# Feed-forward of a hybrid decoder layer: seven-product blocks for gate and up, a spilled hidden layer, and front work put on ScalarE

## Chip, core and metric

One core of one Trainium2 chip runs the whole step as one program. The metric is the device time of one execution in microseconds (us), the median of several. PE is TensorE, PEld its weight loads, DVE is VectorE, ACT is ScalarE, POOL is GpSimd, SP is SyncE, which issues all the DMAs here.

## What is computed

One decoder layer on 1056 tokens (1024 of a prompt, 32 sample tokens), width 1024, all in float32: an input projection, a recurrent branch (convolution of width 4, gated linear recurrence) beside windowed attention, group norms, an output projection, a layer norm, then a gated feed-forward of width 2816 and a second layer norm.

```python
log_a = -LRU_C * r.astype(jnp.float32) * jax.nn.softplus(-lru_lambda.astype(jnp.float32))
a = jnp.exp(log_a)
u = jnp.sqrt(-jnp.expm1(2.0 * log_a)) * (i * x).astype(jnp.float32)
...
h1 = layer_norm(ALPHA * x + y_mix, ln1_g, ln1_b)
hid = jax.nn.silu(jnp.einsum('bsd,df->bsf', h1, w_gate)) * jnp.einsum('bsd,df->bsf', h1, w_up)
ffn = jnp.einsum('bsf,fd->bsd', hid, w_down)
h2 = layer_norm(ALPHA * h1 + ffn, ln2_g, ln2_b)
```

`r` and `i` are sigmoids of two small block products of the convolved `x`.

## The kernel before, in words

**Tokens and tiles.** Activations lie feature-major, [128 features, tokens]. The tokens are two chunks (`SC`): chunk 0 has 512, chunk 1 has 544, and chunk 1 is worked in two blocks of 272 (`BL`), so that a product has 512 or 272 columns. A weight unit is [128, 1024]. Every float32 operand is split into two float32r parts, high and low, and a product is three matmuls (`three`, line 589): high by high, high by low, low by high. One unit against all tokens is thus 8 x 3 x 3 = 72 matmuls, 24 with 512 columns and 48 with 272.

**Splitting a unit.** `split_unit` (line 542) takes each half of a unit, 128x512: a copy to float32r (`copy`, ACT first, DVE possible), and a subtraction for the low part (`tt`, POOL first, DVE possible). A half of a `w_down` unit has its rows' means taken off as well: a sum on DVE, an ACT instruction and a DVE instruction.

**Order.** The program records its instructions, and a list scheduler (`Recorder.order`, line 263) then puts them in the order of issue, by what each costs in a model of its own, by the data and buffers it waits for, and by a latest start worked out backwards from TensorE's order (`deadlines`, line 241). An instruction that two engines can do (`either`, line 204) goes to the first named, unless that would be late and the other is done sooner (`leave`, line 313). Each engine then runs its own list strictly in order; SP too, so a DMA that waits holds up the DMAs behind it.

**Front, lines 606 to 1250.** Projections, recurrence and attention of both chunks, then `out_stream` (line 1222) of chunk 0 and of chunk 1. `attend` (line 849) masks and exponentiates scores, and divides by the sum on DVE (line 878). `recurrence` (line 1046) does the four taps of the convolution on DVE, and adds the gates' biases on DVE (line 1071); `scans` (line 1077) takes the sigmoids, an exponential, a tanh and a square root on ACT. `gate_stream` (line 1129) adds its bias on DVE.

**Middle.** `layer_norm1` (line 1253) normalizes each block, splits the result into `h1` (`finish1`, line 1288), sums it over the features (`add_sum`, line 1244) and takes off the mean, for the second norm. The first three feed-forward tiles (`AHEAD`) are done for chunk 0 alone while chunk 1 is normalized, and afterwards for chunk 1 alone.

**Feed-forward.** `gate_up` (line 1297) does one tile f of 128 hidden features: a gate product into `ps_fg`, silu on ACT, an up product into `ps_fu`, their product on DVE, and a split into `hid`. After each two tiles `down` (line 1331) adds their share of all 8 output tiles to `y1`, through `ps_d`, so that down products lie between gate and up products. All of `h1` and `y1` and a few tiles of `hid` stay in SBUF, in 73 slots of [128, 544] (`NSLOT`). `last_down` and `norm2` (lines 1338 and 1355) finish block by block.

Of the kernel before, what the change touches and what calls it, by code (L numbers as in the profile page):

```python
# [17 lines left out]
P = 128  # L18
# [17 lines left out]
NSLOT2 = 10  # L36
NPR = 4
STEP = 2500
AHEAD = 3
# [13 lines left out]
# ---- a small list scheduler: the kernel below records its instructions; they are issued in the order in which they  # L53
# can run, given what each engine costs per instruction (shapes only), the data they wait for and the free buffers
# [32 lines left out]
class Tag:  # L87
    def __init__(self, pool, kind, cap):
        self.pool, self.kind, self.cap, self.psum = pool, kind, cap, pool.psum
        self.bufs, self.free, self.first = [], cap, 0  # L90

# [58 lines left out]
class Recorder:  # L150
# [5 lines left out]
    def add(self, engine, fn, args, kw, *others):  # L156
        """`others`: (engine, function, args, kw) of instructions that would do the same on another engine"""
# [58 lines left out]
    @contextlib.contextmanager  # L216
    def batch(self):
        """instructions that are to run one after the other: each waits for the data of all"""
        self.group = []
        yield  # L220
        waits = set().union(*(op.before for op in self.group)) - set(self.group)
        for op in self.group:
            op.before |= waits
        self.group = None

    def extra(self, b):
        """how many buffers the instructions recorded before b's may still need beside those in use"""
        t = b.tag
        ev = []
        for c in t.bufs[t.first : b.order]:  # L230
            if not c.taken:
                ev.append((c.start, 1))
                ev.append((c.end + 0.5, -1))
        ev.sort()
        n = peak = 0
        for _, d in ev:
            n += d
            peak = max(peak, n)
        return peak
# [23 lines left out]
    def order(self):  # L263
# [41 lines left out]
        def finish(op, e):  # L305
            """when engine e would be through with op after the more urgent work that waits for it"""
# [17 lines left out]
        def dispatch(e):  # L324
# [34 lines left out]
            for b in op.bufs:  # L359
                if not b.taken:  # L360
                    b.taken = True
                    t = b.tag
                    t.free -= 1
                    while t.first < len(t.bufs) and t.bufs[t.first].taken:
                        t.first += 1
# [62 lines left out]
def cost(engine, fn, outs, ins, args, kw):  # L428
    """ns of an instruction, from its shape"""
# [23 lines left out]
def hybrid_step(ctx: ExitStack, tc: tile.TileContext, xT, w_in, w_gates, w_out, w_g, w_u, w_d, vec, ck, cv, ck_nat,  # L453
# [17 lines left out]
    late = {}  # L471
# [4 lines left out]
    def temp(name):  # L476
        if "pool" in late:
            return late["pool"].tile([P, 512], F32, tag="g2", name=name, bufs=NSLOT2)
# [5 lines left out]
    # ---- constants and small vectors  # L484
    vt = const.tile([P, NVEC], F32, tag="vt", name="vt")
    oi = const.tile([P, 2 * P], F32, tag="oi", name="oi")
    mk = const.tile([P, 2 * P], F32, tag="mk", name="mk")
# [10 lines left out]
    # ---- emission: a queue of matrix work fills the tensor engine between the steps of the other work  # L498
# [16 lines left out]
    def run_filler(stream, step):  # L515
        """emit the stream; after each `step` ns of its matmuls advance the other work"""
# [7 lines left out]
    # ---- weights: a unit is [128, 1024], split exactly into two float32r parts, prefetched in order of use  # L524
# [6 lines left out]
    def load(j):  # L531
        """raw halves of unit j"""
        if state["raw"] == j and j < len(units):
            src, name, _ = units[j]
# [7 lines left out]
    def split_unit(j):  # L542
        if state["part"] == j and j < len(units):
            _, name, halves = units[j]
            if halves:
                h = [slot(f"{name}_h{i}", F32R, HW) for i in range(2)]
                l = [slot(f"{name}_l{i}", F32R, HW) for i in range(2)]
                hs_, ls_ = h, l
            else:
                h = pw.tile([P, D], F32R, tag="wh", name=f"{name}_h", bufs=2)  # L550
                l = pw.tile([P, D], F32R, tag="wl", name=f"{name}_l", bufs=2)
                hs_, ls_ = ([q[:, i * HW : (i + 1) * HW] for i in range(2)] for q in (h, l))
            if halves:
                # less each row's mean over its columns: the second layer norm would take it off their sums
                c = small.tile([P, 4], F32, tag="c", name=f"{name}_c", bufs=3)
                for i in range(2):
                    nc.vector.reduce_sum(c[:, i : i + 1], raws[j][i], axis=mybir.AxisListType.X)
                nc.vector.tensor_scalar(c[:, 2:3], c[:, 0:1], c[:, 1:2], -1.0 / D, op0=ALU.add, op1=ALU.mult)
                for i in range(2):
                    nc.scalar.activation(hs_[i], raws[j][i], AF.Identity, bias=c[:, 2:3])  # L560
                    nc.vector.scalar_tensor_tensor(ls_[i], raws[j][i], c[:, 2:3], hs_[i].bitcast(F32), op0=ALU.add,
                                                   op1=ALU.subtract)
            else:
                for i in range(2):
                    nc.copy(hs_[i], raws[j][i])
                    nc.tt(ls_[i], raws[j][i], hs_[i].bitcast(F32), op=ALU.subtract)
# [3 lines left out]
    def need(i):  # L570
        """unit i; at its first use the next unit is split and the one after that loaded"""
        if i not in seen:
# [5 lines left out]
            if i + 1 < len(units) and units[i + 1][2]:  # L578
                load(i + 2)
                split_unit(i + 2)  # L580
                load(i + 3)
# [3 lines left out]
    def add_unit(src, name, halves=False):  # L585
        units.append((src, name, halves))
# [9 lines left out]
    def block(ps, u, xs, o, n, kts=range(KT)):  # L596
        """one [128, n] block of a projection: unit u against feature-major activations xs"""
# [89 lines left out]
    e_, s_, s2, poly, sp8, nsp8, ab, _ = (sp[:, i] for i in range(8))  # L687
# [4 lines left out]
    bcen = ng2[:, 0:8]  # L692
    def small_vectors():
# [854 lines left out]
```

## Time and profile before

| what | value |
|---|---|
| median of 3 runs | 1209.53 us (1209.03 to 1210.03) |
| span of the profiled execution | 1207.1 us; no other time of it is given |
| PE / PEld busy | 95% / 85% |
| DVE / ACT / POOL busy | 52% / 36% / 41% |
| DMA | 80.42 MB, mean 67 GB/s |

The profile is of one execution. Nearly all instructions carry line 417, the scheduler's issuing line, so a group is told by its tile names: `ps_fg`, `ps_fu`, `ps_d`, `ps_o` are the accumulators of gate, up, down and output products. PE's busy time is modelled: a 272-column matmul is shown as 0.29 us, while the next one starts 0.125 us later. What a matmul costs in a dense row is therefore read from start to start.

### The profile page before, as it was taken

Reading aid. Unit: us, or ns where it says so; the run is one execution under the profiler, and the core shown is the slowest. Engines: PE = TensorE matmul, PEld = TensorE weight load, DVE = VectorE, ACT = ScalarE, POOL = GpSimd, SP = SyncE. Lnnn points to the kernel's source line nnn. Section 1 sums busy time; section 2 is a strip of 40 time slices with the busy share of each in tenths; the row PEclk is TensorE's granted clock in tenths of the full one; section 3 lists DMA queues with packets and bytes.
Section 4 is the critical chain, followed back from the end, with each engine's and each line's share of the span. In section 5 each row is a group of like instructions: output and inputs, shape, how many; then the busy total and the mean of one; then the engine's idle time right before and its main releaser. Section 6 shows DMA issues by size and latency. Waiting matters only on the chain.

```text
span 1207.1 us, 18093 instructions
## 1 busy us (share of the span) xinstructions
PE 1147.1 (95%) x7024; PEld 1023.9 (85%) x7024; DVE 631.5 (52%) x1259; ACT 431.3 (36%) x878; POOL 491.1 (41%) x493
## 2 busy tenths in 40 slices
PE   9788998788888999999999999999999999999996
PEld 7568898776668979999898998989999899999986
DVE  5999889899977577252324142232415132232135
ACT  5375666567545375311120212113021211202135
POOL 6843476666556978412031222203031221303241
PEclk9899999899989999999999999999999999999998
DMA  8410113243121223211011111111111110202004
GB/s 291 136 53 19 41 49 101 65 142 117 63 89 54 80 78 129 90 36 53 26 63 35 53 53 45 44 36 53 36 65 41 53 44 27 70 19 70 1 1 144
DMA packets 48085, 80.42 MB, mean 67 GB/s; under 512 B 8144, under 2 KB 12400, under 8 KB 47984
## 3 DMA queue, kind: packets, MB, share of 16 engines
q1 hardware_dynamic: 48000, 79.27, 19.8%
q8 instruction: 55, 0.90, 0.3%
q14 instruction: 30, 0.25, 0.1%
HBM read 71.98 MB, written 5.58 MB: 64 GB/s over the span
## 4 chain that ended last, share of the span: by engine, by line
PE 73%; DVE 17%; DMA 3%; issue 2%; ACT 2%; POOL 2%; SPq 1%; DVEq 0%; POOLq 0%; ACTq 0%
PE ps_d L417 21%; PE ps_fg L417 20%; PE ps_fu L417 20%; PE ps_o L417 4%; DVE p L417 3%; PE ps_gt L417 3%; DVE xc L417 2%; DVE y L417 1%; DVE yat L417 1%; DVE qst L417 1%; SPq L417 1%; DVE hs L417 1%; DVE pl L417 1%; DMA x_r<-in_dram 1%; DVE v L417 1%
## 5 line engine op out<-in xcount | busy, mean ns | idle before, releaser
L417 POOL TENSOR_TENSOR wg_l<-wg_r,wg_h 128x512 fp32r<-128x512 f32 x50 | 64.8, 1311 | 344.4 <-ACT wg_h L417 344.4
L417 DVE SCALAR_TENSOR_TENSOR y<-y,ps_d 128x272 f32<-128x272 f32 (+1 forms) x240 | 124.9, 521 | 107.2 <-PE ps_d L417 102.5
L417 PE MATMUL ps_fg<-h_h,wg_l 128*128 128x272 f32 (+1 forms) x528 | 171.7, 325 | 0.4 <-POOL wg_l L417 0.4
L417 PE MATMUL ps_fg<-h_h,wg_h 128*128 128x272 f32 (+1 forms) x528 | 171.6, 325 | 0.0
L417 PE MATMUL ps_fg<-h_l,wg_h 128*128 128x272 f32 (+1 forms) x528 | 171.4, 325 | 0.0
L417 PE MATMUL ps_d<-hid_h,wd_l 128*128 128x272 f32 (+1 forms) x528 | 171.3, 325 | 0.0
L417 DVE TENSOR_REDUCE wd_c<-wd_r 128x1 f32<-128x512 f32 x44 | 30.0, 682 | 269.3 <-DMA wd_r<-in_dram 269.3
L417 PE MATMUL ps_fu<-h_h,wu_l 128*128 128x272 f32 (+1 forms) x528 | 170.7, 323 | 0.0
L417 PE MATMUL ps_fu<-h_h,wu_h 128*128 128x272 f32 (+1 forms) x528 | 170.6, 323 | 0.0
L417 PE MATMUL ps_d<-hid_h,wd_h 128*128 128x272 f32 (+1 forms) x528 | 170.6, 324 | 0.0
L417 PE MATMUL ps_d<-hid_l,wd_h 128*128 128x272 f32 (+1 forms) x528 | 170.4, 324 | 0.0
L417 PE MATMUL ps_fu<-h_l,wu_h 128*128 128x272 f32 (+1 forms) x528 | 170.4, 323 | 0.0
L417 POOL TENSOR_TENSOR hid_l<-sg,hid_h 128x272 fp32r<-128x272 f32 (+1 forms) x66 | 63.3, 960 | 126.0 <-ACT hid_h L417 108.3
L417 ACT ACTIVATE sg<-ps_fg 128x272 f32<-128x272 f32 (+1 forms) x66 | 30.5, 463 | 232.4 <-PE ps_fg L417 232.4
L417 PEld LDWEIGHTS ps_fg<-h_h,wg_l 128*128 128x128 f32 x528 | 99.8, 189 | 8.5 <-POOL wg_l L417 0.6
L417 PEld LDWEIGHTS ps_fg<-h_l,wg_h 128*128 128x128 f32 x528 | 99.5, 189 | 7.9
L417 PEld LDWEIGHTS ps_fg<-h_h,wg_h 128*128 128x128 f32 x528 | 99.8, 189 | 7.7
L417 PEld LDWEIGHTS ps_d<-hid_h,wd_l 128*128 128x128 f32 x528 | 99.2, 188 | 8.2 <-issue 0.2
L417 PEld LDWEIGHTS ps_d<-hid_h,wd_h 128*128 128x128 f32 x528 | 99.2, 188 | 8.0 <-issue 0.2
L417 PEld LDWEIGHTS ps_fu<-h_l,wu_h 128*128 128x128 f32 x528 | 99.3, 188 | 7.8
L417 PEld LDWEIGHTS ps_d<-hid_l,wd_h 128*128 128x128 f32 x528 | 99.2, 188 | 7.9
L417 PEld LDWEIGHTS ps_fu<-h_h,wu_l 128*128 128x128 f32 x528 | 99.3, 188 | 7.7
(346 smaller groups left out, 2553.1 us busy)
## 6 DMA issues: line engine op xcount, KB each, us to landing
wg_r<-in_dram SPq DMA_DIRECT2D x50, 256.0 KB, 2.6
wu_r<-in_dram SPq DMA_DIRECT2D x50, 256.0 KB, 2.6
wd_r<-in_dram SPq DMA_DIRECT2D x44, 256.0 KB, 2.6
wo_r<-in_dram SPq DMA_DIRECT2D x32, 256.0 KB, 2.6
wq_r<-in_dram SPq DMA_DIRECT2D x16, 256.0 KB, 3.6
wx_r<-in_dram SPq DMA_DIRECT2D x12, 256.0 KB, 3.5
x_r<-in_dram SPq DMA_DIRECT2D x8, 272.0 KB, 4.6
y<-in_dram SPq DMA_DIRECT2D x8, 272.0 KB, 3.4
```

The costliest lines, as they stand in the source:

```text
L417: getattr(getattr(self.nc, op.eng), op.fn)(*[real(a) for a in op.args], **{k: real(v) for k, v in op.kw.items()})
```

## The change

Two things are done. **Front:** the division in the attention, the first tap of the convolution and the gate branch's bias may now be done by ACT (first named) or DVE. The sigmoids become tanh of half the argument, taken straight from PSUM on ACT with the bias; the formulas after them carry the factors. The product by the square root names POOL first. **Feed-forward:** a pair of tiles, 2 x 128 hidden features, is one block product of 2x2 blocks (features f and f+1; halves of the 1024 inputs; halves of a chunk's tokens), done with seven products and the sums that go with them (`products`). The token-side factors are made once per chunk (`right_factors`), the weight-side ones per pair (`Pair`). All gate and up products come first; `hid` goes to DRAM, and so does the normalized `y1`. The down products follow as a stage of their own (`last_sums`): for each token block, for each half of the outputs, all 22 tiles are accumulated in four banks, and each piece of `w_down` is loaded and split again for each block. `EARLY` = 2 means that one pair is done for chunk 0 alone and then for chunk 1 alone.

```diff
-TABLES = {"Sigmoid": "sigmoid", "Sqrt": "sqrt", "Gelu_apprx_tanh": "gelu", "Silu": "silu", "Exp": "exp"}
+TABLES = {"Sigmoid": "sigmoid", "Sqrt": "sqrt", "Gelu_apprx_tanh": "gelu", "Silu": "silu", "Exp": "exp", "Tanh": "exp"}
...
+    def scaled(p, r):
+        nc.either(("scalar", "activation", (p, p, AF.Identity), dict(scale=r)),
+                  ("vector", "tensor_scalar", (p, p, r, None), dict(op0=ALU.mult)))
...
-            nc.vector.tensor_scalar(pr[:, j, 8 : 8 + w], pr[:, j, 8 : 8 + w], st[:, 4 + j : 5 + j], None, op0=ALU.mult)
+            scaled(pr[:, j, 8 : 8 + w], st[:, 4 + j : 5 + j])
...
-            nc.vector.tensor_scalar(dst, src(0), tap[0], col("conv_b", j), op0=ALU.mult, op1=ALU.add)
+            nc.either(("scalar", "activation", (dst, src(0), AF.Identity), dict(scale=tap[0], bias=col("conv_b", j))),
...
-                nc.vector.tensor_scalar(zz[q][:, o : o + m], ps[:, :m], col(bias, j), None, op0=ALU.add)
+                nc.scalar.activation(zz[q][:, o : o + m], ps[:, :m], AF.Tanh, bias=hbias[:, 4 * q + j : 4 * q + j + 1],
+                                     scale=0.5)
...
+            nc.vector.scalar_tensor_tensor(gi[i], gi[i], 1.0, cut(xcs[i], i[1]), op0=ALU.add, op1=ALU.mult)
...
-            nc.tt(u, u, h, op=ALU.mult, first="vector")
+            nc.tt(u, u, h, op=ALU.mult)
...
+    def right_factors(s):
+        n = SC[s][1]
+        hw = n // 2
+        for k in range(4):
...
+            nc.tt(t1, b11, b12, op=ALU.subtract)
+            nc.tt(t3, b12, b22, op=ALU.subtract)
+            nc.tt(e, t1, b22, op=ALU.add)
+            nc.tt(t4, b21, e, op=ALU.subtract)
+            for nm, r in ((("b21", "b22"), y), (("t1", "e"), u), (("t3", "t4"), v)):
...
+                split((h, l), r[:, :n], 0, n)
...
+    class Pair:
...
+                    p, q = {"s1": ("a21", "a22"), "s2": ("s1", "a11"), "s3": ("a11", "a21"), "s4": ("s2", "a12")}[nm]
...
+                    x = pg2.tile([P, HW], F32, tag="ws", name=f"{self.name}_{nm}", bufs=4)
+                    nc.tt(x, p, q, op=ALU.add)
...
+        def cols(self, nm, k):
+            if nm not in self.parts:
+                h, l = self.parts[nm] = piece(f"{self.name}_{nm}p")
+                x = self.block(nm)
+                nc.copy(h, x)
+                nc.tt(l, x, h.bitcast(F32), op=ALU.subtract)
...
+        def product(i, left, right):
+            for s in chunks:
+                hw = SC[s][1] // 2
+                ps = bank(f"ps_{i}{nm}{s}")[:, :hw]
+                for k in range(4):
+                    yield three(ps, hw, *pair.cols(left, k), *seven[right, k, s], k == 0, k == 3)
+                take(i, ps, *(out[s][a][b] for a in range(2) for b in range(2)))
...
+        for i, left, right in ((1, "a11", "b11"), (6, "s2", "e"), (5, "s1", "t1"), (2, "a12", "b21"), (7, "s3", "t3"),
+                               (3, "s4", "b22"), (4, "a22", "t4")):
+            yield from product(i, left, right)
...
+        yield from products(pairs[1], chunks, f"u{nm}_", blocks(u))
+        for s in chunks:
+            for i in range(2):
+                nc.tt(u[s][i], g[s][i], u[s][i], op=ALU.mult)
+                d = hid[f + i, s] = spill.tile([P, SC[s][1]], F32, tag=f"h{f + i}{s}", name=f"hid{f + i}{s}")
+                nc.sync.dma_start(d, u[s][i])
...
+    def down_piece(f, i, nm):
...
+        nc.sync.dma_start(r, w_d[f][:, i * HW : (i + 1) * HW])
+        h, l = piece(f"wd{f}{i}{nm}")
+        m = wmean[:, f : f + 1]
+        nc.scalar.activation(h, r, AF.Identity, bias=m)
+        nc.vector.scalar_tensor_tensor(l, r, m, h.bitcast(F32), op0=ALU.add, op1=ALU.subtract)
...
+            for f0 in range(0, FT, 2):
+                ws = [down_piece(f, i, f"_{s}{o}") for f in (f0, f0 + 1)]
+                for m in range(4):
+                    c = slice(m * P, (m + 1) * P)
+                    for f, (wh, wl) in zip((f0, f0 + 1), ws):
+                        xh, xl = (x[:, o : o + n] for x in hidden(f, s))
+                        yield three(banks[m], n, wh[:, c], wl[:, c], xh, xl, f == 0, f == FT - 1)
+                if (i, o, f0) == (0, 0, 8):
+                    residual(s)
...
+    streams += [gate_up(f, (0,)) for f in range(0, EARLY, 2)] + [later(settle)]
+    for f in range(0, FT, 2):
+        streams += [gate_up(f, both if f >= EARLY else (1,)), means(f)]
+    streams += [last_sums(*b) for b in LAST]
```

`take` gathers the seven products into the four output blocks: product 1 is copied by ACT, the others are added to or subtracted from blocks in SBUF by DVE, seven instructions per chunk and matrix. `hidden` loads a tile of `hid` back and splits it, once for all its uses; `residual` loads `y1` back, and sums and centers it; `means` loads `w_down` once more for its row means. A ring of four pieces holds split weights (high and low of 128x512 each). In the new second stage the four output banks of a half are finished together.

## Rows read from the trace of the kernel before

**Rows 1.** The page: busy time of each engine, and the chain by engine.

```profile
PE 1147.1 (95%) x7024; PEld 1023.9 (85%) x7024; DVE 631.5 (52%) x1259; ACT 431.3 (36%) x878; POOL 491.1 (41%) x493
...
PE 73%; DVE 17%; DMA 3%; issue 2%; ACT 2%; POOL 2%; SPq 1%; DVEq 0%; POOLq 0%; ACTq 0%
```

**Rows 2.** Windows: span, busy time (and count) by engine, PE clock, DMA share, GB/s.

```profile
0.00:417.00 417.00, 370.05 (x2210) 320.69 (x2210) 350.94 (x722) 237.79 (x503) 265.02 (x287) 0.95 0.29 93
417.00:496.00 79.00, 76.54 (x463) 67.70 (x462) 56.40 (x109) 48.16 (x101) 61.80 (x59) 0.98 0.31 104
496.00:1143.00 647.00, 647.00 (x4029) 588.19 (x4028) 195.57 (x367) 118.52 (x226) 147.18 (x131) 1.00 0.13 45
...
10.00:20.00 10.00, 10.00 (x45) 8.11 (x44) 5.22 (x10) 7.07 (x15) 9.63 (x11) 1.00 1.02 355
```

**Rows 3.** The chain, pieces of the feed-forward: start, us, what.

```profile
489.56 6.04 PE ps_fu L417 x48
...
507.15 11.55 PE ps_fu L417 x72
518.70 23.22 PE ps_d L417 x144
```

**Rows 4.** PE in order of time, around 339 us: start, us, line, operation.

```profile
339.12 0.28 PE L417 MATMUL o<-ph,vst 128*128 128x256 f32 x1
...
339.47 0.28 PE L417 MATMUL o<-pl,vst 128*128 128x256 f32 x1
```

**Rows 5.** The chain of 0 to 417 us, by line.

```profile
by line: PE ps_o L417 12.6%; DVE p L417 9.9%; PE ps_gt L417 9.1%; DVE xc L417 5.6%; issue 4.9%; DVE yat L417 3.0%; DVE qst L417 2.9%; SPq L417 2.8%; DVE hs L417 2.7%; DVE pl L417 2.6%; DMA x_r<-in_dram 2.3%; DVE zz L417 1.9%; PE ps_x L417 1
```

**Rows 6.** Groups by form, DVE and ACT, 0 to 417 us: busy us, mean ns.

```profile
L417 DVE TENSOR_SCALAR p<-p,st 128x256 f32<-128x256 f32 x56 | 34.2, 647 | 0.1
L417 DVE CUSTOM_DVE_ANT_0 p<-s,mk,ng 128x256 f32<-128x256 f32 x56 | 25.5, 474 | 0.8 <-PE s L417 0.7
L417 DVE SCALAR_TENSOR_TENSOR xc<-xr,vt,xc 128x512 f32<-128x512 f32 x24 | 23.9, 996 | 0.2
L417 DVE TENSOR_SCALAR zz<-ps_g,vt 128x272 f32<-128x272 f32 x16 | 7.8, 491 | 0.1
L417 DVE TENSOR_SCALAR xc<-xr,vt 128x512 f32<-128x512 f32 x8 | 7.2, 902 | 1.5 <-ACT xr L417 1.4
L417 DVE TENSOR_SCALAR zz<-ps_g,vt 128x512 f32<-128x512 f32 x8 | 6.0, 744 | 0.1
L417 DVE TENSOR_SCALAR gt<-ps_gt,vt 128x272 f32<-128x272 f32 x8 | 3.9, 492 | 4.9 <-PE ps_gt L417 4.9
...
L417 ACT ACTIVATE p<-p,st 128x257 f32<-128x257 f32 x56 | 28.2, 505 | 6.4 <-DVE st L417 6.3
```

**Rows 7.** Groups by form, all engines, whole span: splitting and evacuating in the feed-forward.

```profile
L417 POOL TENSOR_TENSOR wg_l<-wg_r,wg_h 128x512 fp32r<-128x512 f32 x50 | 64.8, 1311 | 344.4 <-ACT wg_h L417 344.4
L417 DVE SCALAR_TENSOR_TENSOR wd_l<-wd_r,wd_c,wd_h 128x512 fp32r<-128x512 f32 x44 | 35.8, 817 | 21.7 <-PE ps_fu L417 11.6 <-ACT wd_h L417 10.0
L417 ACT ACTIVATE wd_h<-wd_r,wd_c 128x512 fp32r<-128x512 f32 x44 | 30.8, 721 | 97.2 <-PE ps_d L417 88.0 <-DVE wd_c L417 8.9 <-PE ps_fu L417 0.3
L417 DVE TENSOR_REDUCE wd_c<-wd_r 128x1 f32<-128x512 f32 x44 | 30.0, 682 | 269.3 <-DMA wd_r<-in_dram 269.3
L417 DVE TENSOR_TENSOR sg<-sg,ps_fu 128x272 f32<-128x272 f32 x44 | 19.1, 435 | 66.2 <-PE ps_fu L417 66.2
```

**Rows 8.** Groups by form: DVE and POOL instructions whose two inputs lie in SBUF.

```profile
L417 POOL TENSOR_TENSOR wq_l<-wq_r,wq_h 128x512 fp32r<-128x512 f32 x16 | 26.4, 1667 | 0.0
L417 DVE TENSOR_TENSOR sum<-sum,y 128x512 f32<-128x512 f32 x4 | 6.2, 1554 | 1.1 <-POOL sum L417 1.1
L417 DVE TENSOR_TENSOR wu_l<-wu_r,wu_h 128x512 fp32r<-128x512 f32 x2 | 1.4, 692 | 2.1 <-ACT wu_h L417 2.1
```

**Rows 9.** ACT in order of time: the last normalized tiles of chunk 1.

```profile
449.55 1.62 ACT L417 ACTIVATE y<-y,vt 128x272 f32<-128x272 f32 x3
```

**Rows 10.** Who waited for whom on SP's queue, longest first: us, times, longest.

```profile
SPq L417 <- POOL wg_l L417: 336.9, 50, 23.2
```

More of the change, by code (lines that the diff above doesn't have):

```diff
@@ L35 @@
 NSLOT = 73
-NSLOT2 = 10
 NPR = 4
 STEP = 2500
-AHEAD = 3
+EARLY = 2
 WAKE = 16
@@ L228, in extra @@
         t = b.tag
-        ev = []
-        for c in t.bufs[t.first : b.order]:
+        if t.peaks is None:
+            t.peaks = (t.first, [0], [])
+        base, peaks, ends = t.peaks
+        for c in t.bufs[base + len(peaks) - 1 : b.order]:
             if not c.taken:
[L232 to L239, printed above, removed]
+                while ends and ends[0] < c.start:
+                    heapq.heappop(ends)
+                heapq.heappush(ends, c.end)
+            peaks.append(max(peaks[-1], len(ends)))
+        return peaks[max(b.order - base, 0)]
     def deadlines(self):
@@ L543, in split_unit @@
         if state["part"] == j and j < len(units):
[L544 to L566, printed above, removed]
+            _, name = units[j]
+            h = pw.tile([P, D], F32R, tag="wh", name=f"{name}_h", bufs=2)
+            l = pw.tile([P, D], F32R, tag="wl", name=f"{name}_l", bufs=2)
+            for i in range(2):
+                c = slice(i * HW, (i + 1) * HW)
+                nc.copy(h[:, c], raws[j][i])
+                nc.tt(l[:, c], raws[j][i], h[:, c].bitcast(F32), op=ALU.subtract)
             parts[j] = (h, l)
@@ L577, in need, with add_unit @@
             split_unit(i + 1)
[L578 to L581, printed above, removed]
             load(i + 2)
         return parts[i]
-    def add_unit(src, name, halves=False):
-        units.append((src, name, halves))
+    def add_unit(src, name):
+        units.append((src, name))
         return len(units) - 1
@@ L1331, in down @@
-    def down(fs, first):
-        yield 0
-        for m in range(8):
-            for s in range(2):
-                for o, n in BL[s]:
-                    yield from down_block(fs, m, s, o, n, first)
-    def last_down(fs):
-        yield 0
-        for i, (s, o, n) in enumerate(LAST):
-            last = i == len(LAST) - 1
-            var = acc("ps_var", pss, "s") if last else temp(f"var{s}{o}")
-            for m in range(8):
-                yield from down_block(fs, m, s, o, n, False)
-                q = temp(f"q{m}_l2{s}{o}") if m or last else var
-                nc.scalar.activation(q[:, :n], y1[m, s][:, o : o + n], AF.Square)
-                if last:
-                    nc.tensor.matmul(var[:, :n], ones, q[:, :n], start=(m == 0), stop=(m == 7))
-                elif m:
+            while ("b11", 3, s) not in seven:
+                tick()
@@ new lines, in gate_up, with blocks @@
+        g, u = ({s: [slot(f"{x}{f + i}{s}")[:, : SC[s][1]] for i in range(2)] for s in chunks} for x in ("sg", "up"))
+        def blocks(x):
+            return {s: [[x[s][i][:, j * (SC[s][1] // 2) : (j + 1) * (SC[s][1] // 2)] for j in range(2)]
+                        for i in range(2)] for s in chunks}
+        yield from products(pairs[0], chunks, f"g{nm}_", blocks(g))
+        for s in chunks:
+            for i in range(2):
+                nc.scalar.activation(g[s][i], g[s][i], AF.Silu)
@@ new lines, in last_sums @@
+    def last_sums(s, o, n):
+        yield 0
+        last = (s, o, n) == LAST[-1]
+        for i in range(2):
+            banks = []
+            for m in range(4):
+                t, p = next(turn2)
+                banks.append(acc(f"ps_d{i}{m}{s}{o}", p, t)[:, :n])
+            for f0 in range(0, FT, 2):
+                ws = [down_piece(f, i, f"_{s}{o}") for f in (f0, f0 + 1)]
+                for m in range(4):
+                    c = slice(m * P, (m + 1) * P)
[4 more added lines that the diff above has]
+                    residual(s)
+            if i == 0:
+                var = temp(f"var{s}{o}")
+            elif last:
+                var2 = acc("ps_var", pst, "tp")
+                nc.tensor.matmul(var2[:, :n], ones, var[:, :n], start=True, stop=False)
+            for m in range(4):
+                mm = 4 * i + m
+                y = y1[mm, s][:, o : o + n]
+                nc.vector.scalar_tensor_tensor(y, y, ALPHA, banks[m], op0=ALU.mult, op1=ALU.add)
+                q = temp(f"q{mm}_l2{s}{o}") if mm else var
+                nc.scalar.activation(q[:, :n], y, AF.Square)
+                if last and i:
+                    nc.tensor.matmul(var2[:, :n], ones, q[:, :n], start=False, stop=(m == 3))
+                elif mm:
@@ L1360, in norm2 @@
         else:
-            yield
+            for _ in range(4):
+                yield
             r = rstd(var[:, :n], n, f"v2_{s}{o}", 1.0, 1e-5)
```

209 lines of the change are left out of this document (129 added, 80 removed).

## The prediction, made before the changed kernel was run

> **What bounds the kernel now.** I read the page first. PE is busy 95% of the span and makes up 73% of the chain that ended last; DVE makes up 17% of it [rows 1]. The windows say where each of the two counts [rows 2]. From 496 to 1143 us PE is busy all the time at its higher clock level (granted clock 1.00, that is 2.4 GHz), with DVE at 196 of 647 us and POOL at 147: there only fewer or shorter matmuls help. From 0 to 417 us DVE is the fullest of the helpers, 351 of 417 us, against 238 for ACT and 265 for POOL, and PE's mean granted clock is 0.95, so that it fell to its lower level now and then after gaps. In that front PE waits on chains that run through DVE: attention's `p`, the convolution's `xc` and the gates' `zz` are 9.9, 5.6 and 1.9% of the chain there [rows 5]. Between the two, 417 to 496, three tiles are done on both chunks beside the first layer norm.
>
> Last, the dense prices. One unit on all tokens takes 11.55 us (72 matmuls), and on the 544 tokens of chunk 1 6.04 us (48 of 272 columns, so 0.1258 each) [rows 3]. Four matmuls of 256 columns in a row start 0.117 us apart (0.35 us for three steps) [rows 4].
>
> **Gate and up on PE: -59 us.** A pair of tiles of one matrix costs 2 x 11.55 = 23.10 us before. After, seven products of 4 x 3 matmuls are 84 of 256 columns and 84 of 272: 84 x 0.117 + 84 x 0.1258 = 20.40 us. Seven products for eight would give 20.21; the rest is the shorter matmul's fixed part. 2.70 us times 11 pairs times 2 matrices is 59 us. PE's dense time can't fall by more, so the gain ends at -59; the other end depends on whether the helpers keep up, which is the next item.
>
> **Helpers in gate and up: 0, bounds 0 to +26.** One matrix of a pair needs 4 additions and 7 subtractions of 128x512, and half of the 4 products of silu and up: 13 instructions that POOL does first, 13 x 1.311 = 17.0 us of the 20.4 [rows 7]. DVE gathers 14 blocks at 0.435 and takes two row sums at 0.682, 7.5 us; ACT does seven copies, two copies from PSUM and two silus, at 0.5 to 0.7 about 7 us. All of this lies beside PE. It stops being free if POOL's instructions lengthen: in the front, beside a full DVE, POOL's subtraction took 1.667 [rows 8]. 13 x 1.667 = 21.7 us is 1.3 more than PE needs, 26 us over the 20 matrices of pairs on both chunks. I take 0, since DVE would be 37% busy here, nearer to the 30% of the stage where 1.311 was taken than to the front's 84%. The gathered blocks have one input in PSUM, and that form stays at 0.435.
>
> **The transition: +22 us, bounds +7 to +47.** Before, three tiles for chunk 0 (about 33 us of PE work) cover the norm of chunk 1, and 69.3 us of dense work (3 x 23.1) take 79 us, a loss of 9.7 [rows 2, 3]. After, one pair for chunk 0 covers it, 2 x 9.83 = 19.7 us, and the norm is followed by more work: factors with five 272-column and three 544-column instructions for each of four k. The last tile of chunk 1 was normalized at 451.2 us, 34 us after the output products ended [rows 9]. So even with helpers to spare PE waits 34 - 20 us, and some 3 for the first factor: a loss of 17, +7 beside before. The helpers: 44 weight instructions for the two visits of pair 0, 11968 columns of factors (23.4 of 512) and 7.4 of the norm's sums, 74.8 in units of 512 columns. POOL alone needs 98 us, a loss of 57 against the pair's dense 40.8, which is +47. Shared by halves with DVE it depends on whether both go on at once. DVE's own price is 0.692, but its sums beside POOL's sums took 1.554 [rows 8]: they waited for one another. At (1.311 + 0.692)/2 = 1.00 a piece the 74.8 take 75 us, a loss of 34, +24. A little of it can be done before 417, so I take +22.
>
> The Trainium skill bears on this term and speaks against the change: "SBUF — State Buffer", section "Who interferes with whom", says that a DVE instruction with two inputs in SBUF and a GpSimd instruction that reads SBUF exclude each other for a whole instruction. By that rule the sum would have +24 here; if both went on at once, 0.45 a piece, it would have the +7 of the waiting chain.
>
> **The down stage: +11 us, bounds 0 to +68.** PE's work is the same: 23.22 us for two tiles [rows 3]. Mean, addition to `y` after each pair and the center step leave DVE. New is that each piece of weights is made again for each block. In the 272-column blocks two pieces must be made in the 24 matmuls of a step, 24 x 0.1258 = 3.02 us: one ACT instruction of 0.721, then two of DVE at 0.817, 2.4 us before any wait [rows 7]. That fits, with 0.6 to spare, but ACT and DVE also carry the second norm and the splits of `hid`. If each piece cost its ACT and its slowest DVE instruction in series (0.721, and 1.554 as the sums took beside POOL [rows 8]) it would be 2.28 against 1.51, 0.77 us for each of 88 pieces: +68. Nothing below 0, as PE is dense now. I take 0.2 us for each of 44 steps, 9 us, and 2 for the start of the stage. The DMAs: 262 KB in 1.51 us is 174 GB/s; with a tile of `hid` in the same time, 358; the trace has a stretch at 355 [rows 2]. So bandwidth costs nothing by itself. If that cover were gone, `hid` of chunk 1 fetched late, it would add to the first 272-column half only.
>
> **The front: -28 us, bounds +10 to -59.** DVE loses the division (34.2), the first tap (7.2), the gates' biases (13.8) and a part of the gate branch's biases (3.9), some 59 us [rows 6]; the product by the square root, which goes to POOL first, and `gi` times `xc`, which comes to DVE, I set off against each other. If DVE's time bounded the front, -59. ACT gets some 100 instructions (56 + 8 divisions, 8 taps, 24 gates, 12 branch biases) at half a microsecond, as its exponential of the same form takes (0.505), and loses the sigmoids: at most 238 + 50 = 288 us, and DVE would have 351 - 59 = 292. In a front of 390 both would stand near 75%. ACT is in the attention's chain already, so a slower front isn't excluded: +10. For the middle I go by the chain: `p` is 41 us of it, and 34.2 of 59.7 us of `p` are the division: 23 us. Of `xc`'s 23 us the first tap is a quarter, 6. Of `zz`'s 8 some 5. That is 34 us, and the ACT instructions that replace them will still end last in about one case in six: -28.
>
> **The tail: +1 us.** The last four banks end together, so three more additions to `y` at 0.435 precede the last norm.
>
> **Sum.** 1207.1 - 59 + 0 + 22 + 11 - 28 + 1 = 1154 us of span. The median of the runs stands 2.4 us above the profiled span, so **1157 us**.
>
> **Rivals.**
> - *DVE was the front's whole bound.* For it: 351 of 417 us busy [rows 2]. Against: its chain share there is under a third by the groups of [rows 5], the rest being output products, DMAs and issue. The front then gives -59 in place of -28: 1126 us.
> - *Helpers, not PE, set the pace of gate and up.* POOL at 1.667 adds 26 us, and 5 in the transition: 1188 us. For it: 17.0 of 20.4 us is little to spare, and the exclusion of [rows 8]. Against: the gathering instructions of DVE have one input in PSUM, so only splits that the scheduler hands to DVE would collide with POOL's.
> - *The front doesn't move.* The scheduler may leave the division and the taps on DVE (the choice is by its own costs), or PE may wait there for something else: no -28, 1185 us.
> - *The stores of `hid` take the place of PE's waits: slower.* At the end of a pair four stores wait on SP's queue for four POOL instructions (5.2 us). If the loads of the next weights are queued behind, they come 5.2 us late, and a copy and a subtraction follow (0.72 + 1.31): 7.3 us a pair, 80 us over 11 pairs, 1237 us. It decides from 53/11 = 4.8 us a pair on. For it: SP runs in order, and waited 336.9 us for `wg_l` alone [rows 10]. Against: those 336.9 us cost PE nothing, because loads ran ahead, and here raw blocks for two matrices still fit ahead.
>
> **Chances.** Forecast 0.46, front fully DVE-bound 0.12, helper-paced 0.20, front unmoved 0.12, stores 0.10. Only the last is slower than before by over 0.2%, about what a measurement of this kernel can tell from no change; its weak form, near 5 us a pair, gives a little to "same". Faster 0.90, same 0.02, slower 0.08. The range holds the forecast with its bounds, the helper-paced and the unmoved front; the first rival's lower half and the slower one are left out: 1126 to 1196 us.
>
> **What the profile after would show.** Right: gate and up chain pieces of 20.4 us per matrix (168 matmuls), start to start 0.117 and 0.126; down at 23.2 us per two tiles, over all blocks 255 us; DVE well under 84% in the front, which ends near 390; a gap of PE of 10 us or more before chunk 1's first product. Wrong: PE idle inside a pair with a release by POOL (helpers), by a load whose issue followed a store on SP (stores), or by `wd_l` in the 272-column blocks by more than 0.2 us a step (down); a front that still ends after 410. Matmuls of 256 columns clearly over 0.117 us apart would take the gain on PE away, and the forecast with it.

## The result, and the profile of the changed kernel

The changed kernel takes 1178.43 us (median of 4 runs, 1176.85 to 1180.69) beside 1209.62 for the kernel before on the same chip: ratio 0.9748 [0.9731 to 0.9765], 31 us less. The forecast of 1157 us had the direction right and was 21 us too low. The profiled run took 1177.26 us, its span 1175.5.

The page of the changed kernel, busy time of each engine and the chain by engine, against [rows 1]:

```profile
PE 1096.3 (93%) x7546; PEld 1020.7 (87%) x7546; DVE 695.3 (59%) x1332; ACT 569.6 (48%) x1096; POOL 767.0 (65%) x687
...
PE 64%; DVE 7%; issue 1%; ACT 0%; POOL 0%; DVEq 0%; ACTq 0%
```

PE has 51 us less to do, although it issues 522 more matmuls; POOL has 276 us more, ACT 138 and DVE 64 more. Where the differences lie is in the windows below. The two chains can't be set side by side by their shares: the one before reaches back to the start, the one of the changed kernel only to 313 us, so that its shares leave out most of the front. The windows are front, transition, gate and up, down, tail (columns as in [rows 2]).

```profile
0.00:403.00 403.00, 358.18 (x2161) 312.90 (x2162) 311.47 (x636) 259.56 (x562) 253.33 (x285) 0.96 0.33 105
403.00:493.00 90.00, 66.17 (x409) 61.02 (x408) 88.64 (x142) 46.30 (x92) 71.00 (x58) 0.79 0.26 87
493.00:903.00 410.00, 410.00 (x3362) 409.90 (x3361) 145.99 (x341) 130.91 (x233) 346.04 (x271) 1.00 0.35 119
903.00:1162.00 259.00, 259.00 (x1607) 234.67 (x1606) 142.13 (x204) 128.56 (x203) 94.73 (x74) 1.00 0.56 180
1162.00:1175.50 13.50, 2.93 (x16) 2.18 (x14) 7.05 (x12) 4.27 (x9) 1.93 (x2) 0.69 0.24 83
```

Gate and up run dense for 410 us, and so does the down stage, at granted clock 1.00 (2.4 GHz). The one stretch that is not dense is 403 to 493: there DVE is busy 88.64 of 90 us, PE 66, and PE's clock is 0.79 in the mean, so part of the time at its lower level of 1.2 GHz. What releases what there, from the chain of waits in order of time (start us, us, what):

```profile
436.21 2.61 DVE v_d L417 x4
438.96 1.26 PE v_b L417 x2
440.25 2.87 DVE y L417 x8
443.12 4.02 DVE v_d L417 x4
...
474.98 1.80 DVE x_t_l L417
476.79 0.34 DVE up L417
477.13 0.14 issue
477.26 1.94 PE ps_7g L417 x12
...
491.43 1.50 PE ps_4u L417 x12
492.93 2.07 PE ps_1g L417 x17
...
899.98 2.93 PE ps_4u L417 x24
902.90 27.32 PE ps_d L417 x118
```

From the last output products to 477 us the chain is almost all DVE. The first pair on all tokens starts at 492.93, the down stage at 902.90: ten pairs in 409.97 us, 41.0 each, in pieces of 2.9 us for 24 matmuls.

By these marks the 31.6 us between the profiled spans (1207.1 and 1175.5) split as follows. The last output product starts at 416.6 us before and 408.5 after: front -8.

```profile
L417 PE MATMUL ps_o<-mix_h,wo_h x192: 282/289/774, 261.0 to 416.4; 128*128 128x272 f32 x128, 128*128 128x512 f32 x64
L417 PE MATMUL ps_o<-mix_h,wo_h x192: 282/290/1215, 256.2 to 408.3; 128*128 128x272 f32 x128, 128*128 128x512 f32 x64
```

(The lines, before and after, show the first of the three matmuls of a product; the marks take the last, 0.2 us later.) From there to the first dense work on all tokens, at 495.6 before [rows 3], it takes 79.0 us, of which 69.3 are three tiles' dense work; after it takes 84.4, of which one pair's 41.0: 10 us lost before, 43 after, +34. Eleven pairs at 41.0 for 46.2 (4 x 11.55 [rows 3]): -57. Down: 260.2 us after, against 255.4 (eleven times 23.22); the same accounting of the kernel before leaves 5.0 us unexplained in its last stage too, so 0. Tail 12.4 against 12.2. Sum -31.

### The profile page after: what moved, and what is told of

Same layout as the page of the kernel before. It is cut to its first block, busy times and chain, and to the rows that moved or that the text cites. A ratio compares the mean times of both kernels' runs of the same rounds, so it can differ in the third digit from the quotient of the medians.

```text
span 1175.5 us, 20650 instructions
## 1 busy us (share of the span) xinstructions
PE 1096.3 (93%) x7546; PEld 1020.7 (87%) x7546; DVE 695.3 (59%) x1332; ACT 569.6 (48%) x1096; POOL 767.0 (65%) x687
## 4 chain that ended last, share of the span: by engine, by line
PE 64%; DVE 7%; issue 1%; ACT 0%; POOL 0%; DVEq 0%; ACTq 0%
PE ps_d L417 22%; PE ps_o L417 5%; PE ps_7g L417 3%; PE ps_1u L417 3%; PE ps_4g L417 3%; PE ps_6u L417 3%; PE ps_5u L417 3%; PE ps_4u L417 3%; PE ps_3u L417 3%; PE ps_3g L417 3%; PE ps_7u L417 3%; PE ps_2u L417 3%; PE ps_1g L417 3%; PE ps_6g L417 3%; PE ps_5g L417 2%; PE ps_2g L417 2%
## 5 line engine op out<-in xcount | busy, mean ns | idle before, releaser
L417 PE MATMUL ps_d<-hid_h,wd 128*128 128x272 f32 (+1 forms) x1056 | 245.2, 325 | 0.0
L417 PEld LDWEIGHTS ps_d<-hid_h,wd 128*128 128x128 f32 x1056 | 176.7, 188 | 16.0 <-issue 0.5
L417 DVE SCALAR_TENSOR_TENSOR wd<-wd_r,wmean,wd 128x512 fp32r<-128x512 f32 x132 | 116.2, 916 | 107.9 <-ACT wd L417 107.6
L417 PE MATMUL ps_d<-hid_l,wd 128*128 128x272 f32 (+1 forms) x528 | 170.3, 325 | 0.0
L417 ACT ACTIVATE wd<-wd_r,wmean 128x512 fp32r<-128x512 f32 x132 | 90.4, 719 | 93.1 <-PE ps_d L417 83.9
L417 PEld LDWEIGHTS ps_d<-hid_l,wd 128*128 128x128 f32 x528 | 99.0, 188 | 8.4 <-issue 0.5
L417 POOL TENSOR_TENSOR hid_l<-hr,hid_h 128x512 fp32r<-128x512 f32 (+1 forms) x44 | 63.2, 1451 | 11.9 <-ACT hid_h L417 8.8
L417 PE MATMUL ps_o<-mix_h,wo_h 128*128 128x272 f32 (+1 forms) x192 | 66.6, 350 | 1.3 <-DVE y L417 1.3
L417 PE MATMUL ps_o<-mix_l,wo_h 128*128 128x272 f32 (+1 forms) x192 | 63.6, 333 | 0.6 <-POOL mix_l L417 0.6
L417 PE MATMUL ps_o<-mix_h,wo_l 128*128 128x272 f32 (+1 forms) x192 | 63.8, 334 | 0.1
L417 DVE TENSOR_TENSOR up<-up,ps_6u 128x256 f32<-128x256 f32 (+1 forms) x22 | 9.4, 428 | 50.1 <-PE ps_6u L417 46.2
```

Source lines behind the costliest of these rows:

```text
L417: getattr(getattr(self.nc, op.eng), op.fn)(*[real(a) for a in op.args], **{k: real(v) for k, v in op.kw.items()})
```

## Experiments

Ratios are to the kernel before, run on the same chip. The table has two marks of each run's profile: the start of the last output product, and how long from there to the first pair that runs dense on all tokens ("transition").

| kernel | median us | ratio [95%] | last output product | transition |
|---|---|---|---|---|
| after | 1178.43 | 0.9748 [0.9731, 0.9765] | 408.5 | 84.4 |
| front only | 1201.74 | 0.9949 [0.9934, 0.9964] | 409.9 | - |
| feed-forward only | 1182.39 | 0.9783 [0.9768, 0.9798] | 415.5 | 84.0 |
| two pairs ahead | 1195.06 | 0.9889 [0.9869, 0.9909] | 406.1 | - |
| no pair ahead | 1179.50 | 0.9762 [0.9746, 0.9778] | 412.2 | 81.5 |
| fewer factors | 1168.39 | 0.9661 [0.9637, 0.9685] | 408.9 | 73.6 |
| squares on PE | 1181.25 | 0.9778 [0.9754, 0.9803] | 411.3 | 88.9 |
| four direct tiles | 1186.81 | 0.9808 [0.9789, 0.9828] | 410.8 | - |
| two direct tiles | 1184.83 | 0.9799 [0.9784, 0.9813] | 410.3 | 86.0 |
| division on ScalarE | 1161.09 | 0.9623 [0.9602, 0.9644] | 392.5 | 84.3 |
| diagonal on ScalarE | 1169.89 | 0.9692 [0.9676, 0.9707] | 400.8 | 84.7 |
| diagonal and casts | 1173.29 | 0.9714 [0.9685, 0.9744] | 405.7 | 86.2 |
| division and diagonal | 1178.04 | 0.9733 [0.9715, 0.9751] | 404.2 | 88.3 |

**The two halves of the change, each alone.** The first takes the kernel before and makes only the edits of the front; the second takes the kernel after and undoes them.

> The kernel before with the front's edits alone. In the changed kernel the output products end at 402.8 us, against 416.9 before. If that is the front's own gain, and all of it reaches the end, this kernel takes 1209.6 - 14 = 1195 us. Rival: part of the 14 us comes from the new feed-forward, whose norm no longer sums and splits beside the last output products; then the front alone ends later than 403 us and the time is above 1199. The prediction's own term, -28, would give 1182.

> The changed kernel with the front as before. If the two parts add up, and the front is worth 14 of the 31 us, this takes 1178.4 + 14 = 1192 us, with the stretch from the end of the output products to the first pair on both chunks at about 90 us as in the changed kernel. Rival: the old front, with DVE fuller, also delays the factors of chunk 0, so that stretch lengthens beyond 95 us and the time passes 1197.

Alone, the front is worth 6 us and the feed-forward 25; together 31, so they add up. The first text's mark of 402.8 us was a misreading of mine: it is the end of the chain's last long piece of output products, and the last such product starts at 408.5. Its 1195 us and the second text's 1192 rest on that mark, and both missed, by 7 and by 10 us; of the first, the rival's time, above 1199, is what came. The front edits move the mark by 7 to 8 us, not by 28.

**How many pairs run ahead for chunk 0.** Two theories for the transition: H, its length is the helpers' work; C, PE lacks cover, that is, work on chunk 0 while chunk 1 is being normalized.

```
-EARLY = 2
+EARLY = 4     (in the other run: 0)
```

> EARLY 4 in place of 2: two pairs are done for chunk 0 alone, then for chunk 1 alone. Theory H (helpers): the transition of 90 us is set by POOL and DVE instructions with two inputs in SBUF, which exclude one another, and DVE is busy 88.6 of 90 us there. A further pair split over two visits adds 22 such instructions of about 1 us, with more gathering on DVE: no gain, 1178 to 1200 us. Rival C (cover): PE lacks work while chunk 1 is normalized; another 19.7 us of it fills the gap, 1159 to 1165 us.

> EARLY 0: no pair ahead, PE waits through the whole norm of chunk 1, and every pair is done on both chunks. Theory H: 22 weight instructions and the gathering of seven products less for POOL and DVE; the factors of chunk 1 are ready sooner by about 15 to 20 us, nearly what the lost cover costs: 1170 to 1184 us. Rival C: 19.7 us of cover are lost and nothing is won, 1195 to 1200 us.

C's forecasts fail in both runs: more cover costs 17 us, no cover costs nothing measurable. With two pairs ahead each block of weights for them is added up and split twice, and the chain shows those instructions one behind the other on POOL, at a time when the dense stage of the kernel after has begun (chain of waits, two pairs ahead: start us, us, what):

```profile
499.49 1.25 POOL wu_s L417
500.74 1.24 POOL wu_a11p L417
501.98 1.71 POOL wu_s L417
...
553.03 4.94 PE ps_2g L417 x24
```

**Less helper work.** Two of the four factors made from each pair of `y` tiles, and their splits, are left out, and two of the seven products take other factors in their place, so the gate and up values are not the layer's.

```
-            nc.tt(t3, b12, b22, op=ALU.subtract)
-            nc.tt(t4, b21, e, op=ALU.subtract)
...
+            seven["t3", k, s], seven["t4", k, s] = seven["t1", k, s], seven["e", k, s]
```

> The changed kernel without the factors t3 and t4: products 7 and 4 take t1 and e in their place, so the matmuls are the same in number and the values are not the layer's. It leaves out two 272-column additions and one 544-column split for each k and chunk, 8.5 units of 512 columns for POOL and DVE in chunk 1 and 8 in chunk 0. Theory H (POOL and DVE, excluding one another, set the transition at about 1 us a unit): 8 to 12 us less, 1166 to 1171 us. Rival C (cover too short, the chain through the norm sets it): these two factors are the last needed, so nothing is won, 1176 to 1180 us.

```profile
482.48 2.93 PE ps_1g L417 x24
```

The first dense pair starts at 482.5, 10.4 us earlier, and the total falls by as much (0.9748 to 0.9661, 10.5 us). H's forecast came out: this work of the helpers is paid in full.

**Helper work moved to PE.** For chunk 1 the squares of the first norm are summed by PE, in one-column matmuls that accumulate, in place of additions.

```
+            xs_ = parts or [total]
+            for i, x in enumerate(xs_):
+                nc.tensor.matmul(ps[:w, b : b + 1], x[:, b * w : (b + 1) * w], ones[:, 0:1], start=(i == 0),
+                                 stop=(i == len(xs_) - 1))
```

> The changed kernel; for chunk 1 the first norm's squares are summed over the eight tiles by PE (one-column matmuls accumulated in PSUM) in place of 14 additions of 272 columns. 7.4 units less for POOL and DVE; PE gets some 64 small matmuls in a stretch in which it waits anyway. Theory H: 4 to 8 us less, 1170 to 1174 us. Rival C: the additions go on beside the squares on ACT, so the chain is as long as before, 1177 to 1181 us.

No gain: H's 1170 to 1174 us is missed, and C's upper end of 1181 is met by its number. The windows suggest why (columns as before; the kernel after, then this run):

```profile
430.00:440.00 10.00, 7.67 (x38) 7.18 (x38) 9.88 (x17) 2.63 (x7) 7.62 (x6) 0.50 0.36 112
440.00:450.00 10.00, 7.88 (x50) 7.40 (x49) 9.75 (x21) 6.47 (x14) 5.47 (x5) 0.82 0.06 23
```

```profile
430.00:440.00 10.00, 10.00 (x95) 10.00 (x94) 7.21 (x19) 3.12 (x9) 7.29 (x6) 0.62 0.39 131
440.00:450.00 10.00, 10.00 (x64) 9.67 (x64) 4.54 (x17) 3.87 (x9) 1.28 (x1) 0.52 0.00 0
```

PE had been waiting, its clock is near the lower level (0.50 from 430 to 440 us after, 0.62 and 0.52 here), and now PE is the one that is full while DVE and POOL idle. The sums are 128 matmuls here and 16 after; from start to start they take 12.2 us of PE in place of 1.6. That this is what took the gain away is argued from these rows. The profiled execution was also the longest of this kernel's (1186.28 us, median 1181.25), so its marks stand some us later than those of its median run would.

**Tiles that need no factors.** The first four tiles (then two) are computed product by product, from splits of `y` alone, so that PE has work that the factors don't delay.

```
+                    yield three(ps, hw, wh[:, c], wl[:, c], xh, xl, k == 0, k == 7)
...
+    streams += [direct(f, 0) for f in range(EARLY)] + [later(settle)] + [direct(f, 1) for f in range(EARLY)]
```

> The changed kernel; the first four tiles (two pairs) are done as eight plain products, for chunk 0 and then for chunk 1, and pairs begin at the fifth tile. PE's dense work there is 4 x 23.3 = 93 us in place of 82 for two pairs. A plain tile needs 4 split instructions per visit where a pair needs 22, so POOL and DVE have 32 weight instructions, 27.6 units of factors (b12 is split as well) and 7.4 of sums: 67 us of work beside 93 of PE. Theory H: PE waits 10 to 15 us in place of 43, so the time is about 1178 + 11 - 30 = 1159 us (1153 to 1166). Rival: the factors, not the weights, are late, and with them the first pair; then 1168 or more.

> As before with two plain tiles in place of the pair that was split over two visits. The cover is 23 us against 19.7, nearly the same, but POOL and DVE have 16 weight instructions in place of 44. Theory H: about 51 units, the wait of PE falls from 43 to about 20 us, less 5 us for the longer plain products: 1156 to 1164 us. Rival C (cover): the wait stays near 40 us and PE has 5 us more to do: 1178 to 1183 us.

Both of H's forecasts were wrong by more than 20 us. What came is the rival of the first text, late factors; in the second run C's number (1178 to 1183) is nearly met, but not by a lack of cover. PE got its work, ran out of it, and then waited longer. With the factors due later, the kernel's own scheduler left their subtractions on POOL, the engine named first for them, and DVE stood still. DVE in order of time, two direct tiles (in brackets the idle time before, and who ended it):

```profile
449.37 1.17 DVE L417 TENSOR_TENSOR x_b_l<-y,x_b_h 128x544 fp32r<-128x544 f32 x1
466.41 3.09 DVE L417 CAST x_t_h<-rf31u 128x544 fp32r<-128x544 f32 x1 [15.87 <-POOL rf31u L417]
```

With four tiles, DVE and then POOL in order of time:

```profile
475.06 16.68 DVE L417 CAST x_b<-y 128x272 fp32r<-128x272 f32 x1 [21.60 <-POOL rf30v L417]
```

```profile
477.12 0.77 POOL L417 TENSOR_TENSOR x_b<-y,x_b 128x272 fp32r<-128x272 f32 x1
477.84 0.78 POOL L417 TENSOR_TENSOR rf31u<-y 128x272 f32<-128x272 f32 x1
478.56 1.34 POOL L417 TENSOR_TENSOR x_b_l<-y,x_b_h 128x544 fp32r<-128x544 f32 x1
479.85 2.49 POOL L417 TENSOR_TENSOR du_l<-du_r,du_h 128x512 fp32r<-128x512 f32 x2
```

POOL's instructions follow one another without a gap, and a DVE cast of 272 columns is open for 16.68 us beside them; in the kernel after one of 544 columns took 0.43 us at 467.2.

**The front and the transition, by moving work from DVE to ACT.** After, the scheduler had left 23 of the 56 large divisions on DVE. The groups by form of the front, 0 to 409 us, after:

```profile
L417 ACT ACTIVATE p<-p,st 128x256 f32<-128x256 f32 x33 | 16.1, 505 | 8.9 <-DVE st L417 8.6
L417 DVE TENSOR_SCALAR p<-p,st 128x256 f32<-128x256 f32 x23 | 13.8, 609 | 0.3
```

```
     def scaled(p, r):
-        nc.either(("scalar", "activation", ...), ("vector", "tensor_scalar", ...))
+        nc.scalar.activation(p, p, AF.Identity, scale=r)
```

> The kernel after, with the division by the row sums on ScalarE alone (the planner had left 23 of the 56 on VectorE at 609 ns, 33 on ScalarE at 505 ns). Theory F, the front goes as fast as VectorE's list of work: 23 x 0.61 = 14 us leave VectorE, and the last output product, at 408.5 us after, starts 5 to 14 us earlier; total 1164 to 1174 us. Theory L, the front goes by chains of short steps that each have to wait for the one before, whichever engine does them, and by POOL's part of it: the last output product stays within 3 us of 408.5, and the total within 4 us of 1178.4, or longer if softmax waits in ScalarE's queue. L is held the likelier, since the front edits took 40 us of VectorE's busy time and gave 6.

```
-            nc.vector.tensor_scalar(dg[...], ident[:w, :w], r[:, b : b + 1], float(D), op0=ALU.mult, op1=ALU.mult)
+            nc.scalar.activation(dg[...], ident[:w, :w], AF.Identity, scale=r[:, b : b + 1])
```

> The kernel after, with the diagonal that spreads 1/sqrt(variance) over the partitions written by ScalarE (an activation with the factor as its scale, the constant put into the square root) in place of VectorE. Theory D, the stretch from the last output product to the first dense pair is one chain of VectorE instructions that POOL holds up: the two sets of four diagonal pieces take 2.61 and 4.02 us in the chain after, on ScalarE some 1 us each beside VectorE's other work, so the first dense pair starts 4 to 6 us earlier than 492.9 and the total is 1172 to 1176 us. Theory T, the stretch is set by the total of POOL's work and VectorE's two-input work, which share: 6.6 us of VectorE's stretched time were 1 us of work, so the gain is 0 to 2 us, total 1176 to 1179.

```
-                nc.copy(h, x)            (and the two other casts of factors)
+                nc.scalar.copy(h, x)
```

> The run with the diagonal on ScalarE, and the rounding casts of the right factors and of the weight blocks on ScalarE alone too (after, the planner chooses between VectorE and ScalarE; in the chain of the stretch VectorE does four of them, 0.35, 0.83, 1.43 us and one more, and ScalarE is busy 46 of the 90 us there). Theory D: a further 2 to 4 us off the stretch, total 1169 to 1174 us. Theory T: the same as the run with the diagonal alone within 2 us. Against both, if ScalarE's casts wait in line behind its other work: longer than the diagonal alone by 2 us or more, most likely in the front, where the same stretch of program uses none of these casts, so it would show only past 400 us.

The division alone gave 15 us by the ratios (0.9748 to 0.9623), the most of any run: F, the theory I held less likely, is right in sign, and the mark moved by 16 us, above F's upper end of 14 and more than the 13.8 us that DVE had spent on these divisions. The diagonal gave 7 us by the ratios, but not where I looked: its transition takes 84.7 us, as after (84.4), so T is right there; the front lost the time. The norms in the front use the same diagonal, and DVE's 24 pieces there (10.4 us after) went too. The casts added nothing: intervals overlap. The two programs with the diagonal have the same instructions in the same order up to the last output product, and their profiles place it at 400.8 and 405.7. The kernel after, two pairs ahead and squares on PE share one order up to there as well, and have 408.5, 406.1 and 411.3: so much does one profiled front vary.

> The kernel after with both moves to ScalarE that shortened the front: all 56 divisions and all diagonal pieces (the casts as after, since moving them gave nothing). By ratio to before the division alone gave 0.9623 and the diagonal alone 0.9692 against 0.9748 after. Theory F (the front goes as fast as VectorE's list of work, in 0 to 400 us): the two add up, 0.9748 - 0.0125 - 0.0056 = 0.9567, 1153 to 1158 us, the last output product near 385 to 388 us. Theory B (the division has already brought VectorE level with the next limit, ScalarE's own list or POOL's): the diagonal adds less than 3 us, 1158 to 1163 us, and ScalarE's busy share between 100 and 300 us passes 80 of 100. In both the stretch from the last output product to the first dense pair stays at 84 to 86 us, as it did in the kernel after (84.4), with the division (84.3) and with the diagonal (84.7).

Both theories wrong: the gains don't add, they cancel. 1178.04 us is the time of the kernel after. Against the division alone, 12 us are lost before the last output product (404.2 against 392.5) and 4 in the transition (88.3 against 84.3), which both theories had at 84 to 86. In the front the marks say where: up to the last query product (`ps_q`) the runs are equal, 246.8 us here, 247.3 with the division alone, 255.7 after, so 8 to 9 us of gain are there in both. Then, from 250 to 400 us, first the division alone, then both:

```profile
250.00:400.00 150.00, 134.63 (x828) 114.62 (x826) 115.65 (x240) 91.71 (x196) 115.39 (x112) 0.97 0.37 122
```

```profile
250.00:400.00 150.00, 132.07 (x771) 113.64 (x772) 107.64 (x217) 93.12 (x207) 105.73 (x103) 0.91 0.37 117
```

With both moves every helper but ACT is less busy, PE issues 57 matmuls fewer in the same time, at a lower clock. One of the gaps, in the order of PE's instructions with both moves:

```profile
270.88 0.28 PE L417 MATMUL s<-kst_l,qst 128*128 128x256 f32 x1
275.59 0.36 PE L417 MATMUL o<-ph,vst 128*128 128x256 f32 x1 [4.43 <-DVE yat L417]
```

PE stands for 4.4 us at an attention product whose bank DVE has not yet emptied, and the next output product comes after it in PE's order, at 281.2. So the front's time is not the sum of any engine's list. Each edit makes the scheduler write another order, and by these runs an order seems worth more or less by some 10 us. That the order alone is the cause is argued from these rows; writing one run's order into the other was not tried.

The best version measured is the kernel after with all divisions on ScalarE: 1161.09 us, ratio 0.9623 [0.9602, 0.9644].

## Why the prediction was right or wrong, point by point

- **Gate and up on PE, -59: right.** 20.4 us a matrix were forecast, 20.5 measured (41.0 a pair): -57.
- **Helpers in gate and up, 0: right.** PE is busy 410.00 of 410.00 us there. POOL is at 346, as full as the forecast had it, and its instructions took 1.29 to 1.37 us, near the 1.311 I had chosen and not the 1.667 of a busy front. The helper-paced rival is out.
- **The stores of `hid` on SP's queue: refuted.** They do wait on POOL, as the waits of SP's queue from 493 to 903 us show (us, times, longest), and the loads behind them still come in time: PE has no gap.

```profile
SPq L417 <- POOL up L417: 107.4, 40, 4.0
```

- **The transition, +22: mis-sized, +34 measured.** The mechanism was right: the helpers, not the waiting chain, set it, and POOL and DVE shared rather than went on side by side. The price was right too: in the 84.4 us after the last output product POOL and DVE do 102 instructions with two inputs in SBUF, 82.9 in units of 512 columns, so 1.02 us a unit where the forecast had 1.00. What failed is the count, "the 74.8 take 75 us". Of the 82.9, 10.0 are factors of chunk 0, which the sum held to be made by then; chunk 1's factors are 23.4 as forecast, the weights 41, the norm 8.5. These 8 units more, 1.5 us by the price, and the 2 us taken off the sum's 24 make up the 12. Two of chunk 0's late factors and DVE's diagonals, by the groups of 408.5 to 493 us (busy us, mean ns):

```profile
L417 DVE TENSOR_TENSOR rf30v<-y,rf30u 128x256 f32<-128x256 f32 x1 | 1.5, 1497 | 0.0
L417 POOL TENSOR_TENSOR x_t_l<-rf30v,x_t_h 128x512 fp32r<-128x512 f32 x1 | 1.3, 1278 | 0.0
L417 DVE TENSOR_SCALAR v_d<-oi,v_r 68x68 f32<-68x68 f32 x8 | 6.8, 906 | 0.0
```

  Other runs bear the price out: fewer factors has 69.8 units in 73.6 us, the diagonal 83.4 in 84.7, and two pairs ahead 140.9 in the 147 us until its chain leaves the helpers at 553.0. Work that only DVE does (the centering of `y` 6.8 us, the product with the norm's factor 5.9, the diagonals 6.8, the row sums of the down weights 3.9, the gathering of 28 blocks 11.0: 34 us) is not in the sum and was not missed there: with the diagonals moved away the stretch was no shorter. In no run is a unit cheaper than 1.00 us, but four stand clearly above it: no pair ahead (71.3 units in 81.5 us), squares on PE (76.4 in 88.9), division and diagonal (83.4 in 88.3) and two direct tiles (66.4 in 86.0). That chunk 0's factors are the missing part follows from the count; no run moved them alone.
- On the Trainium skill's rule ("SBUF — State Buffer", "Who interferes with whom") that I weighed there, the trace agrees: DVE's subtractions beside POOL took 1.2 to 1.8 us, alone 0.68.

```profile
L417 DVE TENSOR_TENSOR x_t_l<-rf11v,x_t_h 128x544 fp32r<-128x544 f32 x1 | 1.8, 1804 | 0.0
L417 DVE TENSOR_TENSOR wg_a12p<-wg_a,wg_a12p 128x512 fp32r<-128x512 f32 x1 | 0.7, 678 | 0.0
```

- **The down stage, +11: too high, 0 measured.** Both allowances, 0.2 us a step and 2 us for the start, were not needed. The windows show PE busy 259.00 of 259.00 us.
- **The front, -28: wrong, -4 to -8 measured** (by the ratios with and without the front edits 4 to 6, by the marks 7 to 8). The step that failed is "`p` is 41 us of it, and 34.2 of 59.7 us of `p` are the division: 23 us". It took the division to leave DVE whole, and the share of an engine's time in the chain for time that goes with it. First, it did not leave: 23 of 56 divisions stayed on DVE by the scheduler's choice, which I had put as a rival of "doesn't move" at 1185 us and which came close to the truth (1178). Second, the price failed as well. By the prediction's own sum the 33 divisions that left, with the first taps and the biases, were worth some 20 us (an estimate, 33/56 of the 23, and the 6 and 5, less a sixth); 4 to 8 came. The other 23 then gave 16 at the mark, which brings the front to -24 and the time to 1161 us, near the forecast, and 12 of the 16 were lost again when the diagonals were moved as well. So neither 28 nor 8 is the price of these edits; each is that of one order of instructions. DVE lost 40 us of busy time in the front (350.94 [rows 2] to 311.47, in windows 14 us apart in length), and PE's waits changed hands more than they fell (PE's waits until 409 us for `p`, before, then after: us, times, longest):

```profile
PE tp L417 <- DVE p L417: 12.1, 12, 3.6
```

```profile
PE tp L417 <- ACT p L417: 5.3, 4, 2.5
PE tp L417 <- DVE p L417: 5.0, 6, 1.9
```

- **The tail, +1: too small to tell** (12.2 to 12.4).

The two errors around the feed-forward, the transition 12 us too low and the down stage 11 too high, cancel, which is luck; the miss of 21 us is the front's.

## What to carry to other kernels

When a stage between two dense stages is set by helpers that share, count all the work that they still have to do in it, that left over from the stage before too; here the price of a unit was right and 10 units of chunk 0 were the missing part. An instruction's share of a chain does not price what moving it gives. With a list scheduler that writes a new order after each edit, gains of some 10 us in a stage with many short waits neither add up nor last: measure each combination. More cover for a waiting PE did not help here, where the cover was itself work for the engines that PE waited for.

## What the runs showed of the hardware

- A DVE instruction with one SBUF input, too, can stay open long beside POOL: a cast of 128x272 took 16.68 us beside a row of POOL instructions without gaps (one of 128x544 with POOL idle 0.43), and four diagonal pieces of 68x68 took 4.02 us beside POOL (one piece with POOL idle 0.24).
- One-column matmuls on a PE that had been waiting: 128 of them took 12.2 us from start to start, most of them in two windows with a granted clock of 0.62 and 0.52.
- Executions of one order of instructions placed the same product up to 5 us apart (400.8 and 405.7; 406.1, 408.5 and 411.3): a difference of that size in a front like this one needs medians, not single profiles.
